# Splitting 62 of 188 weight chunks by GpSimd's transfers, in a float32 decoder trunk on one core

## The chip, the core and the metric

The kernel runs on one core of a Trainium2 chip. The core has a tensor engine (PE, whose weight loads are shown as PEld), a vector engine (DVE), a scalar engine (ACT), GpSimd (POOL) and SyncE (SP), which here only issues transfers. Each engine works through its own queue in order, and semaphores hold an instruction back until what it reads is there. The metric is device time in microseconds (us), the median of several runs.

## The reference

Two post-norm layers over x of 512 tokens by 1024 features, all in float32. A layer is a token mixer and then a gated feed-forward network, each with a residual and a layer norm:

```python
h = x
for i in range(2):
    mix = s5_mixer(h, ...) if i % 2 == 0 else stick_breaking_mixer(h, ...)
    h = layer_norm(ALPHA * h + mix)
    h = layer_norm(ALPHA * h + (silu(h @ w_g) * (h @ w_u)) @ w_down)     # 1024 -> 2816 -> 1024
# s5_mixer: a diagonal complex state-space layer, y = Re(C s) + D u, then
#   val, gate = split(gelu(y) @ w_glu);  (val * sigmoid(gate)) @ w_out
# stick_breaking_mixer: 16 heads of 64, strictly causal, w_qkv and w_o
```

So the order of the weights is w_glu, w_out (state-space layer), gate, up and down of layer 0, w_qkv, w_o (attention), gate, up and down of layer 1.

## The kernel before

**Products in three parts.** The tensor engine multiplies float32r, a rounded float32. Each operand is kept in two float32r parts, the rounded value (wh, xh) and what is left (wl = w - wh, xl), and a product is three: high by high, low by high, high by low. For the gated unit and the gate and up products they are three lines of the profile in this order: L292 (xh by wh), L293 (xh by wl) and L294 (xl by wh).

**The weight stream.** `Weights` brings all weights in as 188 chunks of 128 x 1024 floats (512 KB), in the order in which they are used: 16 of w_glu, 8 of w_out, 44 gate and up and 22 down of layer 0, the attention's 32, and again 44 and 22. `load` issues a transfer on SP's queue into a slot "raw", three chunks ahead of the split. `pump` splits the next chunk: ACT writes wh, the rounded chunk (L228), and DVE, or POOL in some stretches (`l_eng`), writes wl = raw - wh (L231). The raw slot is then given back. `get(i)` returns chunk i's pair, after pumping two chunks further; `done(i)` gives its slots back. All these tiles come from `Ring`: 37 slots of 4 KB a partition, handed out in the order in which they were given back, so that a new tile waits for the last reader of the tile that had the slot before.

**The state-space layer.** Its steps are written out by hand in one string, `SSM_ORDER`, a letter and a block of 16 channel groups each; every engine's queue follows that order. What matters here: g, t and M make the tables g, transpose them (ACT copies them from PSUM to gt, L637) and multiply them with the input (L647); e makes a block's rotation tables e and r8 (POOL, and ACT at L718); r scans the states into s, whose first columns POOL sets to zero (L745); k makes the intra-chunk kernel table (PE L673, ACT's copy L680, and a POOL addition of the skip term to ksb, L466 in the shared helper); y is the output of a block (L766), from s and from xl; p splits one more weight chunk; u1 is one piece of the gated unit's products (L292 to L294), which are spread between the blocks. The 16 w_glu chunks are used in those pieces and in a part behind the layer's steps, the 8 w_out chunks in `proj`.

**The feed-forward layers.** A hidden tile i of 128 takes two chunks, gate and up (`c_gu[l][i]`), 16 steps of three products; 22 tiles, then 22 down chunks (L311 to L313).

Of the kernel before, what the change touches and what calls it, by code (L numbers as in the profile page):

```python
# [45 lines left out]
def glu_items(text):  # L46
    """Tile and quarters of the GLU's products, a word each; the last two stay in PSUM."""
    first = [(int(w[0]), [int(q) for q in w[1:]]) for w in text.split()]
    keep = [i for i, _ in first[-2:]]
    left = lambda i: [q for q in range(4) if not any(i == t and q in qs for t, qs in first)]  # L50
    order = keep + [i for i, _ in first[:-2] if i not in keep]
    order = list(dict.fromkeys(order))
    order += [i for i in range(8) if i not in order]
    return first, [(i, left(i)) for i in order]
# [5 lines left out]
# the steps of the state-space layer, a letter and a block each (see Trunk.ssm)  # L60
# [5 lines left out]
# blocks whose intra-chunk kernels lie in the second half of xl (0) or xh (1)  # L66
# [7 lines left out]
def rsqrt(nc, tmp, var):  # L74
    """(var + EPS) ** -0.5: a seed from the exponent, then Newton's steps; an instruction at a time, the
    result last."""
    V = nc.vector
    mk = lambda n, t=F32: tmp.tile([128, 1], t, tag=f"rq_{n}", name=f"rq_{n}", bufs=2)
    v, m, i, y, t = mk("v"), mk("m"), mk("i", I32), mk("y"), mk("t")
    V.tensor_scalar(out=v, in0=var, scalar1=EPS, scalar2=None, op0=ALU.add)  # L80
    yield
    V.tensor_scalar(out=i, in0=v.bitcast(I32), scalar1=1, scalar2=None, op0=ALU.logical_shift_right)
    V.tensor_scalar(out=m, in0=v, scalar1=-0.5, scalar2=None, op0=ALU.mult)
    yield
    V.tensor_scalar(out=y.bitcast(I32), in0=i, scalar1=-1.0, scalar2=float(0x5F3759DF), op0=ALU.mult, op1=ALU.add)
    yield
    for _ in range(3):
        V.tensor_scalar(out=t, in0=y, scalar1=y, scalar2=m, op0=ALU.mult, op1=ALU.mult)
        yield
        V.tensor_scalar(out=y, in0=t, scalar1=1.5, scalar2=y, op0=ALU.add, op1=ALU.mult)  # L90
        yield y
# [68 lines left out]
class Ring:  # L160
    """SBUF slots of 4 KB a partition, handed out again in the order in which they were given back."""
# [17 lines left out]
class Packer:  # L179
    """Small float32 tiles, packed into slots."""  # L180
# [17 lines left out]
class Weights:  # L198
    """The weight stream: chunks of 1024 floats a partition, split into two float32r parts."""

    def __init__(self, nc, ring):
        self.nc, self.ring = nc, ring
        self.src, self.raw, self.hl = [], {}, {}
        self.loaded = self.split = 0
        self.nraw = 3
        self.h_eng = self.l_eng = None
# [5 lines left out]
    def load(self, upto):  # L212
        while self.loaded <= min(upto, len(self.src) - 1):
            t = self.ring.get("raw", F32)
            self.nc.sync.dma_start(out=t, in_=self.src[self.loaded])
            self.raw[self.loaded] = t
            self.loaded += 1

    def pump(self, upto):
        nc = self.nc  # L220
        upto = min(upto, len(self.src) - 1)
        while self.split <= upto:
            i = self.split
            self.load(i + self.nraw - 1)
            w = self.raw.pop(i)
            h, l = self.ring.get("wh"), self.ring.get("wl")
            if self.h_eng is None:
                nc.scalar.activation(h, w, AF.Copy)  # L228
            else:
                self.h_eng.tensor_copy(h, w)  # L230
            (self.l_eng or nc.vector).tensor_tensor(out=l, in0=w, in1=h.bitcast(F32), op=SUB)  # L231
            self.ring.put(w)
            self.load(i + self.nraw)
            self.hl[i] = (h, l)
            self.split += 1

    def get(self, i, ahead=2):
        self.pump(i + ahead)
        return self.hl[i]
# [5 lines left out]
class Trunk:  # L245
    def __init__(self, tc, io, ctx):
# [14 lines left out]
        # the order in which the weights are used  # L261
# [17 lines left out]
        self.add_ffn(1)  # L279

# [15 lines left out]
    def fm(self, out, hl, cols=slice(0, S)):  # L296
        """out[128 features, cols] = W^T x, the chunk [128, KD, 128] stationary; a step at a time."""
        wh = hl[0].rearrange("p (k m) -> p k m", k=KD)
        wl = hl[1].rearrange("p (k m) -> p k m", k=KD)
        for k in range(KD):  # L300
            self.mm3(out[:, cols], wh[:, k], wl[:, k], self.xh[:, k, cols], self.xl[:, k, cols], k == 0, k == KD - 1)
            yield

    def tm(self, t, hl, sh, sl, first, last, cols=((0, 512), (512, 1024))):
        """The accumulators [128 tokens, 1024] of token tile t += x W, the chunk [128, 1024] moving."""
        ts = slice(t * 128, t * 128 + 128)
        mm = self.nc.tensor.matmul
        acc = self.ps[:, 2 * t:2 * t + 2].rearrange("p a b -> p (a b)")
        for c0, c1 in cols:
            o, c = acc[:, c0:c1], slice(c0, c1)  # L310
            mm(out=o, lhsT=sh[:, ts], rhs=hl[0][:, c], start=first, stop=False)  # L311
            mm(out=o, lhsT=sh[:, ts], rhs=hl[1][:, c], start=False, stop=False)  # L312
            mm(out=o, lhsT=sl[:, ts], rhs=hl[0][:, c], start=False, stop=last)  # L313
# [3 lines left out]
    # xres = LN(ALPHA xres + y W), and the two parts of its transpose  # L317
# [42 lines left out]
    def tail(self, tiles, nxt, out=None, lag=1, fine=False):  # L360
        """Token tiles one after the other: products (tiles[t], a list of steps), LN, transposes late in
        a following tile's products; nxt starts on the first tokens before the last tile is through."""
# [83 lines left out]
    def ffn_first(self, l):  # L446
        """The first two hidden tiles' products, on some of the tokens."""
# [12 lines left out]
    def ssm(self):  # L460
        """The state-space layer, its GLU and output product. State rows are (half of the groups, p);
        blocks of GB groups of either half give the feature tiles b and 4 + b."""
# [11 lines left out]
        # tables of powers: planes (-im, re, im), entries 0 .. 8  # L474
# [54 lines left out]
        # |lambda|^8; exp(i 8 theta); exp(i 8 theta a), exp(i 64 theta a), 0 <= a <= 8  # L529
# [22 lines left out]
        # coef = (lambda_bar - 1) / lambda  # L552
# [7 lines left out]
        def one(gs):  # L560
            """lambda_bar into the table."""
            t = pwt[gs.start]
            tt(t[:, 1, :, 1], mag[:, gs], cs[:, gs], MUL)
            tt(t[:, 2, :, 1], mag[:, gs], sn[:, gs], MUL)
            V.scalar_tensor_tensor(out=t[:, 0, :, 1], in0=sn[:, gs], scalar=-1.0, in1=mag[:, gs], op0=MUL, op1=MUL)
# [13 lines left out]
        def powers(gs):  # L579
            """Powers of lambda, and their products with coef."""  # L580
# [16 lines left out]
        def outer(o, pw, a, gs, part, sign, ns=slice(0, L)):  # L597
            """A part of o = power * a; with sign -1, a and o are (re, -im)."""
# [30 lines left out]
        def p_t(b, c=0):  # L629
            """Transposes of G's part c."""  # L630
# [9 lines left out]
        def p_m(b, c=0):  # L640
            """v = G x, part c."""
# [9 lines left out]
        def p_d(n):  # L651
            """Products that nothing reads: the tensor engine's clock falls when it waits."""
            for _ in range(n):
                nc.tensor.matmul(out=self.ps[:, 7, 0:128], lhsT=ident, rhs=ident, start=True, stop=True)
# [6 lines left out]
        def p_k(b):  # L661
            """K_t = Re(C lambda^t B), laid by lag into the intra-chunk kernel."""
# [37 lines left out]
        def f_e(b):  # L700
            """exp(i 8 theta c) and |lambda|^8, with a break before each chain."""
# [20 lines left out]
        def f_r(b):  # L722
            """S_c = lambda^8 S_{c-1} + v_c, shifted by a chunk."""
# [73 lines left out]
        def glu(i, qs, banks, start=True, stop=True):  # L797
            """Products of the quarters qs (feature tiles q, 4 + q) of val and gate tile i."""
# [90 lines left out]
    def proj(self, chunks, yt, nxt, order=None, begun=0):  # L889
        """Output product of a mixer, y's transpose in slots (high | low), and its LN."""  # L890
# [24 lines left out]
    def att_q(self, bank, v, st):  # L915
        """q / 8, stacked (high; low) for the pair's first head, (low; high) for its second; k's high
        part twice, and its low part."""
# [32 lines left out]
    def attention(self, st0):  # L950
        """Stick-breaking attention; token rows run backwards in time, so that row r attends to the
        rows after it. weight = sigmoid(z) * prod sigmoid(-z) over the keys in between."""
# [10 lines left out]
        # marks: 1 at key = query + 1  # L963
# [8 lines left out]
        def z_(k):  # L972
# [6 lines left out]
            for qb, off, n in segs:  # L979
                # a matmul of fewer than 192 columns takes longer: 64 unused ones before block 3's  # L980
# [22 lines left out]
        def t_(k, part):  # L1003
            p, u = divmod(k, 3)
            s = st[p]
            if "w" not in s:
# [3 lines left out]
                # columns of key block 0: 128, and 64 of zeros  # L1010
# [131 lines left out]
def cpowers(e, t, ta, tb, neg):  # L1142
    """Entries 2 .. 8 of the table t (planes -im, re, im) from entry 1; -im up to entry 2 neg."""
# [32 lines left out]
def host_layout(x, ssm_a_re, ssm_a_im, ssm_log_dt, ssm_b_re, ssm_b_im, ssm_c_re, ssm_c_im, ssm_d,  # L1176
# [7 lines left out]
    # [f, K, M] -> chunks [f // 128 of pairs, part, 128 rows, K/128 * 128]  # L1184
# [14 lines left out]
    # a quarter: [128 rows, feature tiles q and 4 + q, (val, gate), 128 columns of tile i]  # L1199
# [35 lines left out]
```

## Time and profile before

| | |
|---|---|
| Runs | 1273.69, 1273.86, 1273.94; median 1273.86 us |
| Profiled execution | span 1271.4 us from first to last instruction; its own total isn't listed apart from the three runs, which lie 2.3 to 2.5 us above the span |
| Mean granted TensorE clock | 0.978 |
| SP queue's transfers (30.0% of 16 DMA engines' span) | 116.46 MB |
| Read from memory | 112.38 MB, 92 GB/s over the span |
| Transfers issued by POOL | none |

The page's first parts give busy time by engine and by 40 slices of the span; the groups give, for each line, engine and kind of tile, the busy time, the mean of one and the idle time before them with what ended it. A row of the timeline reads: start, length, engine, line, operation, out<-in, shapes, count, and in brackets the engine's idle time before it and what ended that. A row of the waits reads: engine and line, what it waited for, us in total, times, longest.

### The profile page before, as it was taken

What the parts mean: (1) busy time and instruction counts of PE and PEld (TensorE: products, weight loads), DVE (VectorE), ACT (ScalarE), POOL (GpSimd) and SP (SyncE); (2) the same over time, 40 slices, a digit from 0 to 9 for tenths busy, and PEclk for the clock granted to TensorE, in tenths of its full rate; (3) what the DMA queues carried; (4) which work ended last, traced back from release to release, by engine and by line L of the source; (5) the groups of instructions that cost most, each with busy time, mean ns of one, the idle gap of its engine ahead of it and who ended that gap; (6) DMA issues with size and microseconds to landing.
All of it is one profiled execution on the core that took longest, in us unless ns stands there. A gap on an engine that the chain in (4) does not pass through costs nothing.

```text
span 1271.4 us, 16542 instructions
## 1 busy us (share of the span) xinstructions
PE 1189.0 (94%) x6804; PEld 986.4 (78%) x6804; DVE 691.3 (54%) x1030; ACT 421.5 (33%) x588; POOL 224.2 (18%) x217
## 2 busy tenths in 40 slices
PE   3269899999999999999999999999999999999996
PEld 2157678898888888888897788877988888888885
DVE  8859776772333333322777877877623333333236
ACT  1134344233232222322136666553322222223200
POOL 6982206330000000001024222223300000000000
PEclk9589999999999999999999999999999999999998
DMA  4524474132222223434022112122423222234301
GB/s 135 108 42 86 84 259 139 67 132 84 83 77 73 83 83 105 138 125 130 26 75 61 47 60 67 56 94 100 163 70 99 80 70 83 83 115 139 111 18 50
DMA packets 44332, 117.51 MB, mean 92 GB/s; under 512 B 6368, under 2 KB 17760, under 8 KB 44128
## 3 DMA queue, kind: packets, MB, share of 16 engines
q1 hardware_dynamic: 44256, 116.46, 30.0%
q8 instruction: 53, 0.87, 0.3%
q14 instruction: 23, 0.19, 0.1%
HBM read 112.38 MB, written 4.06 MB: 92 GB/s over the span
## 4 chain that ended last, share of the span: by engine, by line
PE 78%; DVE 5%; ACT 2%; POOL 0%; issue 0%; DMA 0%; DVEq 0%; POOLq 0%; ACTq 0%
PE psum L294 16%; PE psum L292 16%; PE psum L293 16%; PE psum L312 8%; PE psum L311 8%; PE psum L313 8%; DVE nb L999 1%; PE psum L1021 1%; PE psum L1086 1%; PE psum L1088 1%; PE psum L1087 1%; PE psum L1037 1%; PE psum L1036 1%; ACT wh L228 1%; DVE wl L231 1%; PE psum L985 1%
## 5 line engine op out<-in xcount | busy, mean ns | idle before, releaser
L293 PE MATMUL psum<-xh,wl 128*128 128x512 f32 (+1 forms) x1056 | 392.9, 373 | 4.8 <-DVE wl L231 4.8
L292 PE MATMUL psum<-xh,wh 128*128 128x512 f32 (+1 forms) x1056 | 395.0, 375 | 0.7 <-ACT xh L287 0.7
L294 PE MATMUL psum<-xl,wh 128*128 128x512 f32 (+1 forms) x1056 | 394.0, 374 | 0.0
L228 ACT ACTIVATE wh<-raw 128x1024 fp32r<-128x1024 f32 x188 | 194.4, 1054 | 231.1 <-PE psum L313 68.7
L231 DVE TENSOR_TENSOR wl<-raw,wh 128x1024 fp32r<-128x1024 f32 x159 | 198.7, 1279 | 126.3 <-ACT wh L228 98.3
L293 PEld LDWEIGHTS psum<-xh,wl 128*128 128x128 f32 x1056 | 198.8, 188 | 40.9 <-DVE wl L231 5.6
L292 PEld LDWEIGHTS psum<-xh,wh 128*128 128x128 f32 x1056 | 198.6, 188 | 38.4 <-issue 2.4
L294 PEld LDWEIGHTS psum<-xl,wh 128*128 128x128 f32 x1056 | 198.4, 188 | 33.5
L410 DVE TENSOR_TENSOR s<-s,psum 128x512 f32<-128x512 f32 x44 | 30.3, 688 | 278.7 <-PE psum L294 278.7
L231 POOL TENSOR_TENSOR wl<-raw,wh 128x1024 fp32r<-128x1024 f32 x29 | 73.2, 2542 | 456.3 <-DMA raw<-w_v 317.2
L313 PE MATMUL psum<-wh,hid 128*128 128x512 f32 x352 | 137.6, 391 | 0.0
L311 PE MATMUL psum<-wh,hid 128*128 128x512 f32 x352 | 137.4, 390 | 0.0
L312 PE MATMUL psum<-wl,hid 128*128 128x512 f32 x352 | 137.4, 390 | 0.0
L287 ACT ACTIVATE hid<-s 128x512 fp32r<-128x512 f32 x44 | 27.7, 629 | 172.4 <-DVE s L410 172.4
L313 PEld LDWEIGHTS psum<-wh,hid 128*128 128x128 f32 x352 | 66.1, 188 | 14.2
L311 PEld LDWEIGHTS psum<-wh,hid 128*128 128x128 f32 x352 | 66.1, 188 | 13.8
L312 PEld LDWEIGHTS psum<-wl,hid 128*128 128x128 f32 x352 | 66.1, 188 | 13.7
L1000 POOL TENSOR_TENSOR be<-be,nb 128x768 f32<-128x768 f32 (+1 forms) x24 | 49.4, 2059 | 97.9 <-DVE nb L999 82.3
L999 DVE TENSOR_TENSOR_SCAN nb<-nb,dm 128x384 f32<-128x384 f32 (+1 forms) x48 | 49.9, 1081 | 9.7 <-ACT nb L994 6.9
L409 ACT ACTIVATE s<-psum 128x512 f32<-128x512 f32 x44 | 26.2, 595 | 74.4 <-PE psum L294 74.3
L636 PE MATMUL psum<-ident,g 128*128 128x128 f32 x64 | 12.1, 350 | 40.9 <-DVE g L466 20.6
L288 DVE TENSOR_TENSOR hid<-s,hid 128x512 fp32r<-128x512 f32 x44 | 30.5, 693 | 32.2 <-ACT hid L287 32.2
(179 smaller groups left out, 1441.6 us busy)
## 6 DMA issues: line engine op xcount, KB each, us to landing
raw<-w_gu SPq DMA_DIRECT2D x88, 512.0 KB, 3.6
raw<-w_down SPq DMA_DIRECT2D x44, 512.0 KB, 3.6
raw<-w_glu SPq DMA_DIRECT2D x16, 512.0 KB, 4.6
raw<-w_qk SPq DMA_DIRECT2D x16, 512.0 KB, 3.6
raw<-w_out SPq DMA_DIRECT2D x8, 512.0 KB, 4.8
raw<-w_v SPq DMA_DIRECT2D x8, 512.0 KB, 3.6
raw<-w_o SPq DMA_DIRECT2D x8, 512.0 KB, 3.5
xres<-xs SPq DMA_DIRECT2D x4, 512.0 KB, 7.3
```

Source lines behind the costliest of these rows:

```text
L228: nc.scalar.activation(h, w, AF.Copy)
L231: (self.l_eng or nc.vector).tensor_tensor(out=l, in0=w, in1=h.bitcast(F32), op=SUB)
L288: self.nc.vector.tensor_tensor(out=l, in0=src, in1=h.bitcast(F32), op=SUB)
L292: mm(out=out, lhsT=sh, rhs=mh, start=first, stop=False)
L293: mm(out=out, lhsT=sl, rhs=mh, start=False, stop=False)
L294: mm(out=out, lhsT=sh, rhs=ml, start=False, stop=last)
L311: mm(out=o, lhsT=sh[:, ts], rhs=hl[0][:, c], start=first, stop=False)
L312: mm(out=o, lhsT=sh[:, ts], rhs=hl[1][:, c], start=False, stop=False)
L313: mm(out=o, lhsT=sl[:, ts], rhs=hl[0][:, c], start=False, stop=last)
L410: nc.vector.tensor_tensor(out=s, in0=s, in1=self.ps[:, b + 1], op=MUL)
L999: V.tensor_tensor_scan(nb[:, h], nb[:, h], dm[u], 0.0, MUL, ADD)
L1000: G_.tensor_tensor(out=be, in0=be, in1=nb, op=MUL)
```

## The change

For 62 chunks (`by_dma`: all of w_glu and w_out, and the gate and up chunks of tiles 3 to 21 of layer 1) there is no raw slot. POOL issues a transfer of the chunk from memory straight into wh, which rounds it to float32r on the way, at the point at which `load` used to issue on SP. `pump` then has ACT write minus wh into wl, and notes that the rest is due. `rest` issues, also from POOL, a transfer that adds the same chunk, read from memory again, to wl: at the next `pump`, or in `get` when the chunk is due. No DVE or POOL subtraction is left for these chunks. The other 126 go as before. (Comments and docstrings are blanked too.)

```diff
     def load(self, upto):
         while self.loaded <= min(upto, len(self.src) - 1):
-            t = self.ring.get("raw", F32)
-            self.nc.sync.dma_start(out=t, in_=self.src[self.loaded])
+            if self.loaded in self.by_dma:
+                t = self.ring.get("wh")
+                self.nc.gpsimd.dma_start(out=t, in_=self.src[self.loaded])
+            else:
+                t = self.ring.get("raw", F32)
+                self.nc.sync.dma_start(out=t, in_=self.src[self.loaded])
             self.raw[self.loaded] = t
             self.loaded += 1
+
+    def rest(self):
+        for i, l in self.minus:
+            self.nc.gpsimd.dma_start(out=l, in_=self.src[i], accum_op=ADD)
+        self.minus = []
...
             self.load(i + self.nraw - 1)
             w = self.raw.pop(i)
+            self.rest()
+            if i in self.by_dma:
+                h, l = w, self.ring.get("wl")
+                nc.scalar.activation(l, h.bitcast(F32), AF.Copy, scale=-1.0)
+                self.minus.append((i, l))
+                self.load(i + self.nraw)
+                self.hl[i] = (h, l)
+                self.split += 1
+                continue
...
     def get(self, i, ahead=2):
         self.pump(i + ahead)
+        if self.minus and i >= self.minus[0][0]:
+            self.rest()
         return self.hl[i]
...
         self.add_ffn(1)
+        ws.by_dma = set(base) | set(self.c_out) | {c for p in self.c_gu[1][3:] for c in p}
```

The changed kernel's lines stand some 23 further down (L660 is before's L637, L768 before's L745, L489 before's L466); L218 is the rounding transfer, L240 ACT's negation, L227 the accumulate. Names end in numbers of the tile.

**The first chunk.** ACT's queue in the early state-space layer, before (wh_38 is chunk 0's high part):

```order
L680 ACTIVATE ksb_22_411<-psum_67 128x512
L637 ACTIVATE gt_30_466<-psum_67 128x512 x2
L228 ACTIVATE wh_38_493<-raw_35_487 128x1024
L718 ACTIVATE r8_43_501<-pk_5_93 128x16x63
L637 ACTIVATE gt_46_515<-psum_67 128x512 x2
L774 ACTIVATE ysb_47_600<-psum_67 128x4x8x16 x2
```

The same place of ACT's queue now (wl_38 is chunk 0's low part, wh_35 its high part):

```order
L703 ACTIVATE ksb_22_411<-psum_67 128x512
L660 ACTIVATE gt_30_466<-psum_67 128x512 x2
L240 ACTIVATE wl_38_493<-wh_35_487 128x1024
L741 ACTIVATE r8_42_499<-pk_5_93 128x16x63
L660 ACTIVATE gt_45_513<-psum_67 128x512 x2
L797 ACTIVATE ysb_46_598<-psum_67 128x4x8x16 x2
```

ACT's order is the same; its source is now a transfer that POOL issues. POOL's queue around that point, before (s_29 is block 0's states, e and eu block 1's rotation tables):

```order
L1144 TENSOR_TENSOR scr_1_79<-pk_5_93 128x2x96 x2
L1144 TENSOR_TENSOR pk_5_93<-scr_1_79 128x48x4
L745 MEMSET s_29_460 128x16
L466 TENSOR_TENSOR e_41_499<-pk_5_93,pk_4_90 128x512
L466 TENSOR_TENSOR eu_42_500<-pk_5_93,pk_4_90 128x512
```

And POOL's queue there now:

```order
L1167 TENSOR_TENSOR scr_1_79<-pk_5_93 128x2x96 x2
L1167 TENSOR_TENSOR pk_5_93<-scr_1_79 128x48x4
L768 MEMSET s_29_460 128x16
L218 DMA wh_35_487<-w_glu 128x1024
L218 DMA wh_36_489<-w_glu 128x1024
L218 DMA wh_37_491<-w_glu 128x1024
L218 DMA wh_39_495<-w_glu 128x1024
L489 TENSOR_TENSOR e_40_497<-pk_5_93,pk_4_90 128x512
L489 TENSOR_TENSOR eu_41_498<-pk_5_93,pk_4_90 128x512
```

The first four chunks' transfers moved from SP's queue, where nothing stood ahead of them, to behind POOL's power tables and the memset of s.

**The middle of the layer.** POOL's queue before, from block 1's kernel table (ksb_52) to block 2's (ksb_86):

```order
L466 TENSOR_TENSOR ksb_52_691<-pk_2_80,ksb_52_691 128x4x16
L745 MEMSET s_60_729 128x16
L466 TENSOR_TENSOR e_71_821<-pk_5_93,pk_4_90 128x512
L466 TENSOR_TENSOR eu_72_822<-pk_5_93,pk_4_90 128x512
L466 TENSOR_TENSOR e_71_821<-pk_5_93,pk_4_90 128x512
L466 TENSOR_TENSOR eu_72_822<-pk_5_93,pk_4_90 128x512
L466 TENSOR_TENSOR e_71_821<-e_71_821,eu_72_822 128x512 x2
L719 MEMSET r8_73_823 128x16
L466 TENSOR_TENSOR ksb_86_1048<-pk_2_80,ksb_86_1048 128x4x16
```

POOL's queue now from block 1's kernel table on (wl_38 and wl_54 are the low parts of chunks 0 and 1):

```order
L489 TENSOR_TENSOR ksb_51_689<-pk_2_80,ksb_51_689 128x4x16
L227 DMA wl_38_493<-w_glu 128x1024
L218 DMA wh_55_717<-w_glu 128x1024
L768 MEMSET s_58_726 128x16
L227 DMA wl_54_715<-w_glu 128x1024
L218 DMA wh_65_810<-w_glu 128x1024
L489 TENSOR_TENSOR e_68_817<-pk_5_93,pk_4_90 128x512
```

The accumulate of chunk 0 now stands directly behind that addition. POOL's queue around block 2's kernel table (wl_64, wl_78 and wl_88 are chunks 2, 3 and 4, wh_145 a w_out chunk):

```order
L227 DMA wl_64_808<-w_glu 128x1024
L218 DMA wh_79_950<-w_glu 128x1024
L218 DMA wh_145_1758<-w_out 128x1024
L489 TENSOR_TENSOR ksb_82_1043<-pk_2_80,ksb_82_1043 128x4x16
L227 DMA wl_78_948<-w_glu 128x1024
L218 DMA wh_89_1085<-w_glu 128x1024
L227 DMA wl_88_1083<-w_glu 128x1024
```

Chunk 3's accumulate stands behind the addition, and that behind a w_out load. POOL's queue around block 3's kernel table (wl_101 is chunk 5):

```order
L218 DMA wh_142_1721<-w_out 128x1024
L218 DMA wh_140_1716<-w_out 128x1024
L227 DMA wl_101_1236<-w_glu 128x1024
L218 DMA wh_104_1244<-w_glu 128x1024
L489 TENSOR_TENSOR ksb_105_1310<-pk_2_80,ksb_105_1310 128x4x16
```

The accumulates stand between POOL's own steps: behind a kernel table's addition, or behind a load whose slot another engine has to give back first (wh_145's by DVE's u, wh_140's by the last products of block 3's kernel table).

**The last layer.** POOL's queue had no rows there before. Now, from the load of a tile on (wl_642 and wl_644 are tile 4's low parts, wh_668 is the high part of a later tile):

```order
L218 DMA wh_665_7670<-w_gu 128x1024
L218 DMA wh_668_7705<-w_gu 128x1024
L227 DMA wl_642_7383<-w_gu 128x1024
L227 DMA wl_644_7412<-w_gu 128x1024
L218 DMA wh_670_7734<-w_gu 128x1024
L227 DMA wl_647_7447<-w_gu 128x1024
```

Each accumulate stands behind a load, and that load waits until PE gives the slot back.

More of the change, by code (lines that the diff above doesn't have):

```diff
@@ L205, in __init__ @@
         self.nraw = 3
+        self.by_dma, self.minus = set(), []
         self.h_eng = self.l_eng = None
```

## The prediction

> **What bounds the kernel now.** I read the page first: the engines' shares and the row of slices.
>
> ```profile
> span 1271.4 us, 16542 instructions
> PE 1189.0 (94%) x6804; PEld 986.4 (78%) x6804; DVE 691.3 (54%) x1030; ACT 421.5 (33%) x588; POOL 224.2 (18%) x217
> PE   3269899999999999999999999999999999999996
> ```
>
> TensorE is 94% busy; its idle time lies in the first six or so of 40 slices, the state-space layer. Next the busy time by stage (columns: length, busy time of PE, PEld, DVE, ACT, POOL with counts, then clock, DMA share, GB/s).
>
> ```profile
> 81.00:172.00 91.00, 81.40 (x990) 62.98 (x992) 75.84 (x59) 42.24 (x60) 27.38 (x23) 0.96 0.49 101
> 960.00:1100.00 140.00, 140.00 (x613) 114.85 (x613) 46.28 (x50) 39.75 (x52) 0.00 (x0) 1.00 0.27 83
> ```
>
> From 960 to 1100 (the last feed-forward layer) PE never stops and DVE works 46.28 of 140 us: no relief of DVE can be worth anything there. From 81 to 172 PE leaves 9.6 us idle and DVE is 83% busy. So the whole effect is decided by what PE waits for before about 172 us. Those waits are:
>
> ```profile
> PE psum L766 <- POOL s L745: 11.4, 1, 11.4
> PE psum L293 <- DVE wl L231: 4.8, 2, 4.3
> PE psum L766 <- DVE s L466: 2.7, 2, 1.9
> ```
>
> Only the last two rows are waits for DVE; together 7.5 us is the most that less DVE work in this stage could give.
>
> **What is taken away.**
>
> ```profile
> L228 ACT ACTIVATE wh<-raw 128x1024 fp32r<-128x1024 f32 x188 | 194.4, 1054 | 231.1 <-PE psum L313 68.7
> L231 DVE TENSOR_TENSOR wl<-raw,wh 128x1024 fp32r<-128x1024 f32 x159 | 198.7, 1279 | 126.3 <-ACT wh L228 98.3
> raw<-w_glu SPq DMA_DIRECT2D x16, 512.0 KB, 4.6
> xres<-xs SPq DMA_DIRECT2D x4, 512.0 KB, 7.3
> L215 SPq DMA_DIRECT2D raw<-w_glu x16: 327/387/497, 42.1 to 178.7; - x16
> 190.59 2.42 POOL L231 TENSOR_TENSOR wl<-raw,wh 128x1024 fp32r<-128x1024 f32 x1 [26.20 <-DVE wl L231]
> ```
>
> 62 of 188 chunks lose their subtraction: 52 on DVE (159 become 107; 52 x 1.28 = 66 us of DVE) and 10 on POOL (10 x 2.42 = 24 us). ACT keeps 188 passes of the same shape, which now write minus the rounded chunk. SP loses 62 loads; POOL gains 124 transfers, and each of the 62 chunks is read from memory twice, +32.5 MB. The last layer reads 83 GB/s now. While its gate and up chunks pass it would read at most twice that, 166.
>
> **The unknown prices.** No transfer from POOL's queue is in this trace, so two durations and one issue time are bounded.
> - The rounding transfer, issue to landing. The nearest row is a plain load of the same 512 KB from the same tensor; its landings here were:
>
> ```profile
> DMA to landing us min/median/max: 3.3/4.5/9.5
> ```
>
>  I take the median, 4.5 us, bounds 3.3 and 9.5.
> - The accumulate. It reads the tile back besides reading memory; I put it midway between that median and the slowest kind on the page, the 7.3 us of the xres load: 5.9 us, same bounds.
> - POOL's time to issue one: between SP's 0.33 us and the 2.42 us that POOL takes to go over the whole tile; I take 1.0, nearer to the issue row, since an issue doesn't touch the data.
>
> **Place A, the first chunk.** Before, ACT rounds chunk 0 at 50.75, from a load at 42.1 us. Now its source is a transfer that stands in POOL's row directly behind the memset of s.
>
> ```profile
> 50.75 1.05 ACT L228 ACTIVATE wh<-raw 128x1024 fp32r<-128x1024 f32 x1
> 51.69 1.03 ACT L718 ACTIVATE r<-pk 128x1008 f32<-128x1008 f32 x1
> 54.30 0.60 ACT L637 ACTIVATE gt<-psum 128x512 f32<-128x512 f32 x1 [0.26 <-PE psum L636]
> 55.05 1.98 PE L647 MATMUL psum<-xres,gt 128*64 128x64 f32 x32
> 71.45 0.12 POOL L745 MEMSET s<- 128x16 f32 x1
> 71.63 1.12 PE L766 MATMUL psum<-h,s 64*64 64x128 f32 x8 [11.43 <-POOL s L745]
> 72.68 0.69 PE L766 MATMUL psum<-xl,xres 128*64 128x128 f32 x4
> 88.00 1.07 ACT L637 ACTIVATE gt<-psum 128x512 f32<-128x512 f32 x2
> ```
>
> ACT's queue is in order: behind the pass over chunk 0 stand r8 and the two copies to gt, PE's block-1 products wait for gt, and y0 stands behind them on PE. All of this used to be over by 57 us, in the shadow of the memset at 71.45; now it starts there. 71.57 + 4.5 landing = 76.1; pass 0.94 (51.69 - 50.75) 77.0; r8 1.0, 78.0; two gt copies 1.07, 79.1; products 1.98, 81.1; the part of y0 that needs only xl and xres 0.69, 81.8. y0 started at 71.63: 10.1 late, less 0.8 that I allow because some of the products overlap the second copy. **A: +9.3 us.** The four issues also put POOL's e tables 4 us back, less than PE's own delay.
>
> **Place B, the first gated-unit product.** The accumulate of chunk 0 stands behind the kernel-table addition ksb on POOL.
>
> ```profile
> 86.58 0.58 ACT L680 ACTIVATE ksb<-psum 128x512 f32<-128x512 f32 x1
> 87.24 1.10 POOL L466 TENSOR_TENSOR ksb<-pk,ksb 128x64 f32<-128x64 f32 x1 [1.24 <-ACT ksb L680]
> 88.38 0.39 PE L293 MATMUL psum<-xh,wl 128*128 128x512 f32 x1
> 128.68 0.39 PE L294 MATMUL psum<-xl,wh 128*128 128x512 f32 x1
> 128.91 0.40 PE L292 MATMUL psum<-xh,wh 128*128 128x512 f32 x1
> 133.62 0.80 PE L293 MATMUL psum<-xh,wl 128*128 128x512 f32 x1 [4.32 <-DVE wl L231]
> 137.05 0.39 PE L292 MATMUL psum<-xh,wh 128*128 128x512 f32 x1
> ```
>
> ksb ends at 88.34 and PE's product with wl is at 88.38: there is no slack. 88.34 + 5.9 = 94.24, 5.9 us of waiting. A pause also costs afterwards: behind the 4.32 us one, eight products took 3.43 us (133.62 to 137.05), against 0.23 from one to the next at full pace (128.68 to 128.91): 3.43 - 1.84 = 1.6. **B: +7.5.**
>
> **Place C.** y1's wait for DVE goes, since DVE runs ahead by four subtractions.
>
> ```profile
> 104.69 0.94 PE L766 MATMUL psum<-h,s 64*64 64x128 f32 x8 [1.89 <-DVE s L466]
> ```
>
> **C: -1.9.**
>
> **Place D, chunks 3 and 4.** POOL first issues a w_out load into a slot that DVE's u gives back, then ksb, then chunk 3's accumulate.
>
> ```profile
> 121.35 0.80 POOL L466 TENSOR_TENSOR ksb<-pk,ksb 128x64 f32<-128x64 f32 x1 [16.03 <-ACT ksb L680]
> 121.89 1.34 DVE L466 TENSOR_TENSOR u<-pk,bb 128x1024 f32<-128x1024 f32 x1
> 123.64 0.39 PE L293 MATMUL psum<-xh,wl 128*128 128x512 f32 x1
> ```
>
> u ends at 123.23; + 1.0 + 0.8 + 5.9 = 130.9 against 123.64: 7.3, and 1.6 for the pace. In return the 4.3 us stall at 133.62 and its 1.6 go (chunk 4's accumulate is issued right behind, in the new wait). **D: +3.0.**
>
> **Place E, chunk 5.** POOL issues a w_out load whose slot comes free only with PE's last products of block 3's kernel tables, and chunk 5's accumulate stands behind it.
>
> ```profile
> 151.78 0.57 PE L673 MATMUL psum<-h,g 64*32 64x112 f32 x16
> 155.65 0.50 PE L293 MATMUL psum<-xh,wl 128*128 128x512 f32 x1 [0.49 <-DVE wl L231]
> 170.61 0.94 PE L766 MATMUL psum<-h,s 64*64 64x128 f32 x8 [0.81 <-DVE s L466]
> ```
>
> 152.35 + 1.0 + 5.9 = 159.25 against 155.65: 3.6 + 1.6. **E: +5.2.** The wait of 0.81 at 170.61 is DVE's: **F: -0.8.** From there PE has a backlog, and the later chunks are split ahead.
>
> **The last layer.** Each gate-and-up tile of 16 x 3 products takes about 11 us (48 x 0.23). POOL's queue there holds, word for word in the order of rows, a rounding load that waits for the products of tile i-2 to end, then the accumulates of tile i.
>
> ```profile
> 934.13 1.99 ACT L228 ACTIVATE wh<-raw 128x1024 fp32r<-128x1024 f32 x2
> 943.82 0.39 PE L293 MATMUL psum<-xh,wl 128*128 128x512 f32 x1
> ```
>
> The first of ACT's two passes over tile 4 ends at about 935.2, PE wants the tile at 943.82: 8.6 us for the accumulate, against 5.9. And four issues a tile may take 2.75 us each before POOL is the bound. **Term: 0**; the cover is those 8.6 us, and if it is gone, the excess comes 18 times.
>
> **The sum.** 9.3 + 7.5 - 1.9 + 3.0 + 5.2 - 0.8 = +22.3: span 1271.4 becomes 1293.7. Between span and reported time lie 2.5 us (median 1273.86), so about 1296. The places are added as if POOL's and ACT's rows shift along with PE; every one is anchored to an event of the same chain.
> Low ends (3.3, 3.3, 0.33, no pace loss): 8.1 + 3.3 - 1.9 - 0.3 + 0.3 - 0.8 = +8.7, 1282.6. High ends (9.5, 9.5, 2.42): 14.3 + 11.1 - 1.9 + 8.0 + 10.2 - 0.8 = +40.9, 1314.8, and (9.5 - 8.6) x 18 = 16 more in the last layer, 1331.
>
> The Trainium skill, "DMA: Bandwidth & Descriptors", section "Anatomy of one DMA — SWDGE (gpsimd) path", fits a transfer from GpSimd's queue as about 2.0 us plus its bytes over 436e3 per us; for 524,288 bytes that is an estimate of 3.2 us for either transfer. By it the sum would be 8.0 + 3.2 - 1.9 + 0.3 + 0.9 - 0.8 = +9.7, about 1283.6, the second rival below. The trace's plain loads never landed under 3.3 and at the median took 4.5, so I hold it for a floor.
>
> **Rivals.**
> - *The accumulates don't keep up in the last layer* (0.17). Each us above 8.6 costs 18 us there; at 10 us: 1.4 x 18 = 25, and 4.1 more at B, D and E each, 12.3: 1273.9 + 22.3 + 12.3 + 25 = about 1333. For it: the bytes of two reads, a read back and a write, and the 9.5 us that a plain load has taken. Against: in that layer the DMA engines are 27% busy.
> - *The transfers are quick* (0.10): all near 3.3 us, about 1283. Place A remains, because it comes from the row order, not from the length of a transfer. Against: w_glu's median of 4.5 in that very stage.
> - *The relief of DVE decides* (0.03 faster, 0.02 the same). The waits for wl and s (4.3, 0.5, 1.9, 0.8 and 1.6 of pace) go, 9.1 us: about 1265. That needs chunk 0 rounded before ACT reaches it at 50.75, so issued by about 46; POOL's row puts it after 71.45. It turns to a gain where A, B, D and E cost under 9 together; A alone at its low end is 8.1.
>
> **How the numbers follow.** The forecast has 0.68. The predicted time is its sum, 1296; its own range is 1282 to 1315. The range for 8 in 10 goes on to 1326, into the first rival, leaving out the rest of that rival (about 0.12) and the last one. A difference under 0.2%, 2.5 us, can't be told from none. Slower: 0.68 + 0.17 + 0.10 = 0.95; same 0.02; faster 0.03.
>
> **What the changed profile would show.** A: a wait of y0's group (or of the block-1 products before it) for ACT's gt, and chunk 0's rounding issued near 71.6; if it is issued before 50, A falls. B, D, E: PE's L293 products waiting for a DMA into wl near 98, 140 and 170 us, of 4 to 8 us each. C, F: no waits for s at L766. Last layer: PE without gaps for 140 us in a stretch behind 980; a gap of the same size in each of 18 tiles shows the first rival. The prediction is wrong if the accumulate lands outside 3.3 to 9.5 us, if POOL's issue is above 2.42, or if POOL's rows wait on something that I haven't followed.

## The result, and the profile after

The changed kernel takes 1314.62 us (median of 4 runs, 1313.23 to 1315.76) against 1273.78 for the kernel before beside it: ratio 1.0321, 95% interval 1.0309 to 1.0334. That is 40.8 us slower; the forecast was 22 slower, with this time just inside the high end of its range (1282 to 1315). The page of the changed kernel:

```profile
span 1312.5 us, 16633 instructions
PE 1196.7 (91%) x6804; PEld 991.9 (76%) x6804; DVE 621.5 (47%) x978; ACT 420.9 (32%) x588; POOL 283.9 (22%) x331
...
DMA  4318779923222222344320212213477787864301
...
q0 software_dynamic: 17856, 65.02, 21.6%
q1 hardware_dynamic: 35328, 83.95, 21.6%
...
wh<-w_gu POOLq DMA_DIRECT2D x38, 512.0 KB, 6.0
wl<-w_gu POOLq DMA_DIRECT2D x38, 512.0 KB, 7.1
wh<-w_glu POOLq DMA_DIRECT2D x16, 512.0 KB, 7.0
wl<-w_glu POOLq DMA_DIRECT2D x16, 512.0 KB, 10.2
...
wh<-w_out POOLq DMA_DIRECT2D x8, 512.0 KB, 12.7
```

DVE has 70 us less work, and the kernel is slower all the same. The row of DMA shares has a plateau that wasn't there before: 8 7 7 9 9 in slices 4 to 8 (from about 98 to 262 us), and 7s and 8s in the last layer. POOL's 124 transfers (q0) occupy the 16 transfer engines for 21.6% of 1312.5 us, 2.29 us each on average; SP's transfers before took 30.0% of 1271.4 for 116.46 MB, 1.72 us for each 512 KB. The last column of the issues is the median from issue to landing: 6 to 13 us, where the plain loads of weights took 3.5 to 4.8 in the kernel before.

TensorE's waits (engine and line, what it waited for, total, times, longest):

```profile
PE psum L670 <- ACT gt L660: 23.4, 1, 23.4
...
PE psum L316 <- DMA wl<-w_glu: 17.4, 3, 7.0
PE psum L335 <- DMA wl<-w_out: 10.0, 1, 10.0
```

The first row takes the place of the old 11.4 us wait for POOL's memset; it begins earlier on PE, so only part of it is new. The three waits for wl<-w_glu are the forecast's places B, D and E. The wait for w_out has no counterpart in the forecast. The rows of PE's timeline at these places:

```profile
80.98 1.12 PE L789 MATMUL psum<-h,s 64*64 64x128 f32 x8
104.77 0.79 PE L316 MATMUL psum<-xh,wl 128*128 128x512 f32 x1 [5.56 <-DMA wl<-w_glu]
145.99 0.80 PE L316 MATMUL psum<-xh,wl 128*128 128x512 f32 x1 [7.04 <-DMA wl<-w_glu]
179.18 0.80 PE L316 MATMUL psum<-xh,wl 128*128 128x512 f32 x1 [4.84 <-DMA wl<-w_glu]
265.34 0.80 PE L335 MATMUL psum<-wl,zt 128*128 128x512 f32 x1 [9.99 <-DMA wl<-w_out]
```

PE issues the same 6804 products in both kernels, in the same order but for two, so each product's start can be set against its start before. How far the changed kernel lies behind, by place, is worked out from the two traces. "Pace" is what PE loses in slower products behind a pause: behind the wait that ends at 104.77 the granted clock was 0.50 from 104.8 to 109.6, and 1.00 again from 110 on.

| Place | start before | start after | behind | forecast | measured |
|---|---|---|---|---|---|
| A, block 0's output | 71.63 | 80.98 | 9.4 | +9.3 | +9.4 |
| up to the first gated-unit product | 88.03 | 98.36 | 10.3 | 0 | +1.0 |
| B, chunk 0's low part | 88.38 | 104.77 | 18.7 with pace | +7.5 | +8.4 |
| C, block 1's output | 108.76 | 124.24 | 15.5 | -1.9 | -3.2 |
| D, chunk 3, and chunk 4's old wait gone | 136.78 | 155.43 | 18.7 | +3.0 | +3.2 |
| E, chunk 5 | 155.65 | 179.18 | 26.0 with pace | +5.2 | +7.3 |
| F, block 3's output | 170.61 | 197.12 | 26.5 | -0.8 | +0.6 |
| to the last of the gated unit | 206.62 | 235.60 | 29.0 | 0 | +2.5 |
| G, w_out | 226.09 | 265.34 | 41.6 with pace | 0 | +12.6 |
| from there to the end | | | 41 | 0 | 0 |

The two products that moved are of the gated unit, stood behind block 3's output before and stand ahead of it now. They lie in the row of F and hide its gain: from the products of block 3's output that need no s (169.36 before) to those that do (170.61) PE gains 0.9.

The windows show the stage of G and the last layer (columns as in the prediction; a packet counts whole where it starts, so the share of a full stretch can read a little over 1). First the end of the state-space layer in the kernel before, then the changed kernel:

```profile
182.00:236.00 54.00, 54.00 (x238) 44.34 (x237) 36.61 (x35) 28.42 (x34) 28.83 (x12) 1.00 0.48 174
```

```profile
205.00:265.00 60.00, 47.87 (x210) 38.15 (x208) 20.39 (x28) 28.27 (x36) 18.23 (x21) 0.96 1.07 289
...
1000.00:1100.00 100.00, 100.00 (x439) 82.14 (x438) 12.42 (x18) 28.14 (x36) 24.36 (x33) 1.00 0.78 169
```

From 205 to 265 the DMA share is 1.07: the transfer engines are full, and PE is idle for 12.1 us. The last w_out chunk shows both its transfers late: its rounding load, issued at 240.38, lands at 253.89, and its accumulate, issued at 255.32 behind ACT's negation, at 265.30. In the last layer the engines are 78% busy, against 27% before, and PE never stops.

### The profile page after: what moved, and what is told of

The parts are those of the page before. It is cut to its first block, busy times and chain, and to the rows that moved or that the text cites. A ratio compares the mean times of both kernels' runs of the same rounds, so it can differ in the third digit from the quotient of the medians.

```text
span 1312.5 us, 16633 instructions
## 1 busy us (share of the span) xinstructions
PE 1196.7 (91%) x6804; PEld 991.9 (76%) x6804; DVE 621.5 (47%) x978; ACT 420.9 (32%) x588; POOL 283.9 (22%) x331
## 3 DMA queue, kind: packets, MB, share of 16 engines
q0 software_dynamic: 17856, 65.02, 21.6%
q1 hardware_dynamic: 35328, 83.95, 21.6%
## 4 chain that ended last, share of the span: by engine, by line
PE 77%; POOL 6%; DVE 6%; issue 5%; DMA 4%; ACT 3%; SPq 0%; DVEq 0%; POOLq 0%; ACTq 0%
PE psum L317 15%; PE psum L316 15%; PE psum L315 15%; PE psum L335 8%; PE psum L336 8%; PE psum L334 8%; POOL scr L1167 2%; DVE nb L1022 1%; DMA wh<-w_out 1%; PE psum L789 1%; PE psum L1044 1%; POOL pk L1167 1%; DMA wl<-w_glu 1%; PE psum L1109 1%; DMA wl<-w_out 1%
## 5 line engine op out<-in xcount | busy, mean ns | idle before, releaser
L316 PEld LDWEIGHTS psum<-xh,wl 128*128 128x128 f32 x1056 | 200.4, 190 | 54.4 <-DMA wl<-w_glu 18.7
L248 ACT ACTIVATE wh<-raw 128x1024 fp32r<-128x1024 f32 x126 | 131.9, 1057 | 224.3 <-PE psum L336 68.4
L251 DVE TENSOR_TENSOR wl<-raw,wh 128x1024 fp32r<-128x1024 f32 x107 | 134.8, 1286 | 107.0 <-ACT wh L248 79.1
L251 POOL TENSOR_TENSOR wl<-raw,wh 128x1024 fp32r<-128x1024 f32 x19 | 47.6, 2522 | 411.8 <-DMA raw<-w_v 317.2
L240 ACT ACTIVATE wl<-wh 128x1024 fp32r<-128x1024 f32 x62 | 62.7, 1046 | 50.2 <-DMA wh<-w_glu 38.0
L659 PE MATMUL psum<-ident,g 128*128 128x128 f32 x64 | 13.0, 370 | 42.2 <-DVE g L489 20.6
L227 POOL DMA_DIRECT2D wl<-w_gu x38 | 33.8, 899 | 77.2 <-ACT wl L240 75.1
## 6 DMA issues: line engine op xcount, KB each, us to landing
wl<-w_glu POOLq DMA_DIRECT2D x16, 512.0 KB, 10.2
wh<-w_out POOLq DMA_DIRECT2D x8, 512.0 KB, 12.7
```

The costliest lines, as they stand in the source:

```text
L240: nc.scalar.activation(l, h.bitcast(F32), AF.Copy, scale=-1.0)
L316: mm(out=out, lhsT=sl, rhs=mh, start=False, stop=False)
```

## Experiments

**The last layer alone.**

```diff
-ws.by_dma = set(base) | set(self.c_out) | {c for p in self.c_gu[1][3:] for c in p}
+ws.by_dma = {c for p in self.c_gu[1][3:] for c in p}
```

> Only the 38 gate and up chunks of the last layer are split by transfers; w_glu and w_out go as before. Theory (the whole loss lies before 275 us, the accumulates of the last layer land within their 8.6 us): 1273.8, within 1 us of the kernel before, no wait of TensorE for a low part between 940 and 1185 us. Rival (the last layer costs something that the delays don't show, its POOL queue or its doubled reads): 1277 to 1290.

1273.02 us, ratio 0.9996 (0.9987 to 1.0005): no difference, as forecast. The window of the last layer in this run, to be read beside the row of the kernel before that the prediction shows:

```profile
960.00:1100.00 140.00, 140.00 (x613) 114.99 (x612) 17.95 (x26) 39.78 (x52) 31.33 (x43) 1.00 0.79 175
```

DVE's work there falls from 46.28 to 17.95 us and the time doesn't move. Relieving an engine that has slack was worth nothing here, and the price, transfer engines at 79% where they were at 27%, is hidden too.

**Without w_out.**

```diff
+ws.by_dma = set(base) | {c for p in self.c_gu[1][3:] for c in p}
```

> The 8 w_out chunks go back to SP's loads and to subtractions; all else is as changed. Theory (the last w_out chunk's accumulate costs 10.3 us and 2.4 of pace at its products, and a w_out load ahead of chunk 3's accumulate on POOL costs 2 at the third wait): 1314.6 - 12.7 - 2 = 1300. Rival (the transfer engines are so full from w_glu alone that the same wait comes at another chunk): 1308 to 1315.

1307.73 us (1.0269, 1.0254 to 1.0285): 6.9 us come back, half of what the theory said, and just below what the rival said. The wait of 10.0 is gone and D's wait is 2 us shorter as expected (5.1 for 7.0), but new waits stand in its place (rows of PE's waits):

```profile
PE psum L316 <- DMA wl<-w_glu: 16.9, 5, 5.3
PE psum L804 <- ACT ysb L797: 3.9, 2, 3.2
...
PE psum L334 <- ACT wh L248: 2.0, 1, 2.0
PE psum L335 <- POOL wl L251: 1.9, 1, 1.9
```

E stays (a wait of 4.95), although no w_out load stands ahead of chunk 5's accumulate any more. The transfer engines are still full (a share of 0.97 from 175 to 205 us and of 1.02 from 205 to 235).

**Without chunk 0.**

```diff
+ws.by_dma = set(base[1:]) | set(self.c_out) | {c for p in self.c_gu[1][3:] for c in p}
```

> Chunk 0 alone goes back to SP's load, ACT's rounding and DVE's subtraction; the other 61 are as changed. Theory (both the late start of block 0's output, 9.4, and the first gated-unit product's wait, 6.1 with 2.3 of pace, belong to this one chunk, with some 1 us between them): 1314.6 - 18.7 = 1296, block 0's output at 71.6 again. Rival (the delay of the first part hides another one behind it, such as later chunks that come no earlier): less than 10 us gained, 1305 or more.

1298.94 us (1.0199, 1.0185 to 1.0213), 15.7 back. Block 0's output starts at 71.26 again, and the first gated-unit product doesn't wait: one chunk of 62 held A and B. Of the 3 us that are missing to 18.7, 1.55 are a wait for chunk 1, at 96.18, that chunk 0's had hidden; the rest isn't put down to one place.

**Half of the late accumulates' bytes.** The second half of these low parts is left at minus the high part.

```diff
-            self.nc.gpsimd.dma_start(out=l, in_=self.src[i], accum_op=ADD)
+            n = 512 if 8 <= i < 24 else 1024
+            self.nc.gpsimd.dma_start(out=l[:, :n], in_=self.src[i][:, :n], accum_op=ADD)
```

> The accumulates of chunks 8 to 23 (half of w_glu, all of w_out) add only the first 512 of 1024 columns: half of their bytes, the same queues and the same order; the other half of these low parts stays at minus the high part. Theory S (from 205 to 265 us the 16 transfer engines are full, so the last w_out accumulate waits for others): 4.2 MB less at some 285 GB/s is 14.7 us of their time, so the wait of 10.0 for the last w_out chunk falls to under 3: 1302 to 1305. Theory Q (it is late because its load is issued late, behind slots and POOL's order): the wait stays at 8 or more, 1311 to 1314.

1299.66 us (1.0209, 1.0192 to 1.0226): 15.0 back, somewhat more than theory S said. The order on every queue is unchanged, and A, B, D and E are as in the changed kernel; PE's list of waits has none for w_out, and the same window reads:

```profile
205.00:265.00 60.00, 60.00 (x268) 49.16 (x267) 29.15 (x38) 30.38 (x37) 24.66 (x23) 1.00 0.84 233
```

PE is busy for all 60 us as soon as the transfer engines aren't full (0.84). So G is the transfer engines' throughput, not the place in a queue; theory Q falls.

**The accumulate at once.**

```diff
                 self.minus.append((i, l))
+                self.rest()
```

> The accumulate of a chunk is issued right behind ACT's negation of it, not at the next pump; the same 62 chunks. Theory (the waits for low parts of chunks 0 and 3 come from where the accumulate stands in POOL's queue): chunk 0's now stands ahead of block 1's rotation tables and lands by 85, so its wait of 5.6 with 2.3 of pace goes; chunk 3's stands ahead of the w_out load and the kernel table, so its 7.0 with 2.3 goes, but chunk 4 (behind a part addition) waits some 4 to 6 as in the kernel before; the late start of 9.4, chunk 5's wait (ACT's late negation) and the w_out wait stay: 1300 to 1304. Rival (the length of the transfers decides, not their place): 1311 to 1315.

1317.58 us (1.0341, 1.0315 to 1.0366), no gain, and above the range of theory and rival alike. The waits at B and D are gone (at the product that started at 133.62 before, the kernel is 8.0 us behind, where the changed kernel is 20.2), so their cause, the place in POOL's queue, is borne out. But from 155 to 178 us on before's scale this kernel falls from 10 to 30 us behind, where the changed kernel falls from 19 to 26: some 13 us come on top. At w_out a wait of 8.2 stays. Two rows of POOL's timeline in that stretch:

```profile
193.61 0.89 POOL L227 DMA_DIRECT2D wl<-w_glu  x1 [9.13 <-ACT wl L240]
194.21 0.85 POOL L218 DMA_DIRECT2D wh<-w_glu  x1
```

An accumulate at once waits at the head of POOL's queue for ACT, and the next chunk's load stands behind it; the kernel that put the accumulate a step later let the load go first. Here that load landed at 201.00, and PE, which had waited 5.6 us for it, went on at 201.13. How much of the other 7 us is such order and how much is full transfer engines wasn't separated.

**Two or three chunks, early accumulate.** Both have the line of the run before, and:

```diff
+ws.by_dma = {base[2], base[4]}        # the first;  set(base[2:5]) the second
```

> Only chunks 2 and 4 of w_glu are split by transfers, the accumulate right behind the negation; everything else as in the kernel before. Theory (a few chunks, loaded ahead and away from the first product, take DVE off the path): the wait of 4.3 with 1.6 of pace for chunk 4 shrinks to 0 to 3, and block 1's output waits less for DVE (1.9): 1266 to 1271. Rival (POOL's queue makes new waits even with two): 1274 or more.

> As the run with chunks 2 and 4, with chunk 3 too. Theory: chunk 3's accumulate, ahead of block 2's kernel table on POOL, lands before its product, and DVE has one subtraction less: 1265 to 1270, equal to the run with two within 2. Rival (chunk 3's product waits as in the changed kernel, since its negation is late on ACT): 1274 to 1279.

1279.86 (1.0046, 1.0031 to 1.0061) and 1279.61 (1.0043, 1.0026 to 1.0060): some 0.5% slower, outside the theory in both runs. The rival of the first (POOL's queue makes new waits) fits; in the second chunk 3 didn't wait, so its rival isn't the cause. The first loss is not a wait for a transfer: block 1's output waits 3.9 us for DVE's s, 1.9 before. POOL's accumulate of chunk 2 waited for ACT until 100 us, the rotation tables stood behind it, and they then ran at the same time as DVE's additions of s. DVE's timeline and POOL's, with chunks 2 and 4:

```profile
100.83 7.95 DVE L490 TENSOR_TENSOR s<-s,w 128x504 f32<-128x504 f32 x2
```

```profile
100.00 0.90 POOL L227 DMA_DIRECT2D wl<-w_glu  x1 [10.35 <-ACT wl L240]
100.60 1.45 POOL L490 TENSOR_TENSOR e<-pk,pk 128x512 f32<-128x512 f32 x1
```

**The same two, accumulate at the next pump; and chunks 1, 2, 4.** The accumulate stands as in the change.

```diff
+ws.by_dma = {base[2], base[4]}        # the first;  {base[1], base[2], base[4]} the second
```

> Chunks 2 and 4 alone by transfers, the accumulate at the next pump as in the change (it stands behind the rotation tables of block 3 on POOL, not ahead of them). Theory (in the run with the early accumulate, POOL's tables were held until 100 us and then ran beside DVE's additions of s, which took 7.95 instead of 1.28): the tables run at 88 to 99 again, DVE's additions take 1.3, block 1's output isn't late, and chunk 4 waits 2 to 4 instead of 4.3: 1271 to 1274. Rival (it is the transfers themselves that slow DVE): 1278 to 1281 again.

> Chunks 1, 2 and 4 by transfers, accumulates at the next pump. Theory: with chunk 1's subtraction gone DVE reaches block 1's states 1.2 earlier and its wait of 1.9 goes, chunk 1's product waits some 1.8 for its accumulate, chunk 4 waits 2 to 4 instead of 4.3 and 1.6: 1269 to 1273, level with the kernel before or under it by up to 0.4%. Rival (chunk 1's accumulate or the tables behind it make a larger wait): 1275 or more.

1275.09 (1.0013, 1.0004 to 1.0022) and 1276.51 (1.0025, 1.0016 to 1.0035), the first 1 us above its theory's range, the second in its rival's. With chunks 2 and 4, POOL's tables are out of the way in time and the additions take their usual length:

```profile
104.07 1.28 DVE L489 TENSOR_TENSOR s<-s,w 128x504 f32<-128x504 f32 x2
```

The row is DVE's timeline with chunks 2 and 4. Block 1's output is on time, as the theory said, and some 4.5 us of the loss are back. What is left is chunk 4, whose accumulate POOL issues behind a part addition (row of PE's timeline with chunks 2 and 4):

```profile
134.24 0.80 PE L316 MATMUL psum<-xh,wl 128*128 128x512 f32 x1 [6.20 <-DMA wl<-w_glu]
```

PE waits 6.2 us, where DVE's subtraction cost 4.3 and the theory said 2 to 4. With chunk 1 as well, chunk 1's accumulate costs 1.7, as the theory said, but the wait for chunk 4 is 6.7. No version with transfers in the state-space layer beat the kernel before, and the last layer alone is level with it.

**Without chunks 0, 3, 5 and w_out.**

```diff
+ws.by_dma = set(base) - {base[j] for j in (0, 3, 5)} | {c for p in self.c_gu[1][3:] for c in p}
```

> Chunks 0, 3 and 5 of w_glu and all of w_out go back to SP, ACT and DVE; 13 w_glu chunks and the last layer's 38 stay with the transfers. Theory (the loss is at the first chunk, the three accumulates that are late, and the w_out stage): all five are gone, and 1.8 for chunk 1 and some pace stay: 1270 to 1278. Rival (other chunks become late in their place, since the transfer engines are full from 175 us on and a later accumulate stands in the same row): 1282 to 1292.

1291.02 us (1.0141, 1.0127 to 1.0155), in the rival's range. At the product of 153.26 (before) this kernel is 0.3 us behind, so what A, B and D cost is gone. From there to 247 us it loses 18 us, in waits of 3.4 for a late accumulate (at 164.86), 3.4 for ACT's ysb (at 190.44), and smaller ones, with the pace behind them, while the transfer engines are full from 160 to 205:

```profile
160.00:205.00 45.00, 37.50 (x209) 27.95 (x208) 9.61 (x7) 13.62 (x16) 14.51 (x14) 0.89 0.96 245
```

Then the same with the accumulates of chunks 6 to 15 halved (their second half stays at minus the high part):

```diff
+            n = 512 if 6 <= i < 24 else 1024
+            self.nc.gpsimd.dma_start(out=l[:, :n], in_=self.src[i][:, :n], accum_op=ADD)
```

> As the run without chunks 0, 3, 5 and w_out, but the accumulates of chunks 6 to 15 add only the first 512 of 1024 columns: the same instructions in the same order on every queue, 2.6 MB less to move; the other half of these low parts stays at minus the high part. Theory S (the 18 us lost between 160 and 247 us are the transfer engines' throughput): 2.6 MB at some 300 GB/s is 8.7 us, so 6 to 10 us come back: 1281 to 1285. Theory Q (they come from the order on POOL's and ACT's queues, in which the accumulates wait for other engines): 1288 to 1292.

1285.01 us (1.0097, 1.0076 to 1.0118): 6.0 us back, the low end of what S said, with every queue's order the same; the distance behind at the end of that stretch falls from 18.0 to 11.9. So traffic is part of it. Waits of 1.7 for an accumulate, 2.0 for a rounding load, 1.5 for ACT's ysb and 1.9 for a subtraction on POOL remain, and how much of these is traffic too stays open.

## Why the prediction was right, and where it fell short

- **What bounds the kernel, and what DVE's relief is worth: right.** The last layer's term of 0 was measured alone at 0.9996. Its cover of 8.6 us was enough: the accumulates there took 7.1 at the median; 6 of 38 took more than 8.6, up to 11.2, and PE didn't stop for them either. Four issues a tile took 2 x 0.55 + 2 x 0.88 = 2.9 us of 11 (rows below), so POOL never came near its bound. One reading is short: the same view of PE's waits before has 20.6 us for DVE's g (L636), which the prediction leaves out of the waits for DVE. They are 20.6 in the changed kernel too, so the sum doesn't suffer.

```profile
L218 POOL DMA_DIRECT2D wh<-w_gu x38: 527/551/1297, 920.5 to 1128.5; - x38
L227 POOL DMA_DIRECT2D wl<-w_gu x38: 860/880/1292, 941.5 to 1164.8; - x38
```

- **A: right in place and size** (9.4 for 9.3). Chunk 0's rounding was issued at 71.66 and ACT's pass over it began at 76.13, forecast 76.1; without that chunk the term is gone.
- **B, D: right in place, close in size.** The accumulates for which PE waited were issued at 97.86 and 139.58 and PE went on at 104.77 and 145.99: 6.9 and 6.4 us, where 5.9 was taken. The early accumulate removed both. The pace behind a pause cost 2.3 and not 1.6 each.
- **E: right in place and nearly in size, wrong in what ends last.** The w_out load did wait for PE's products of block 3's table until 171.53, but chunk 5's accumulate, issued at 173.86, waited for ACT's negation, which ran later still:

```profile
171.53 0.53 POOL L218 DMA_DIRECT2D wh<-w_out  x1 [8.99 <-PE psum L696]
173.86 0.89 POOL L227 DMA_DIRECT2D wl<-w_glu  x1 [1.80 <-ACT wl L240]
```

 Without any w_out load, the wait was still there.
- **C and F: both gains came**, C with 1.4 of pace on top, F with 0.9 (hidden in its row by the two products that moved).
- **The step that failed** is the sentence behind F, "From there PE has a backlog, and the later chunks are split ahead." It took POOL's transfers one by one, each with a landing time, and never summed what they ask of the 16 engines. With that it held that the whole effect is decided before about 172 us; G's product started at 226 before. By the shares of the two pages of the profile, 48 transfers of 2.29 us are 110 us of all 16 engines in the state-space layer, in place of 24 x 1.72 = 41, and 44 of them come late, between 98 and 265 us. From 205 to 265 the engines are full, an accumulate issued at 255.32 lands at 265.3, and w_out costs 12.6 us that the forecast has at 0. Halving the late accumulates' bytes alone took it away. With 3.5 more at E and F, 2.5 behind them and some 0.8 in sum at the other places, this is the difference between 22.3 and 41.6.
- **The landing bound of 9.5 us was too low.** The median was 10.2 for w_glu's accumulates and 12.1 for w_out's, and the longest took 20.1 (row of the full list of issues):

```profile
wl<-w_out POOLq DMA_DIRECT2D x8, 512.0 KB, 12.1
```

 An accumulate outside 3.3 to 9.5 us is one of the prediction's own signs of being wrong. The high end of the sum, 1314.8, met the result by another way than its own: it had B, D and E longer, and the trace has them as forecast, with G on top. So the range held by luck, not for the reasons given for its upper part, and the sum itself, 22.3, has little more than half of the 41 us.
- By the page of the Trainium skill that the prediction weighed ("DMA: Bandwidth & Descriptors", "Anatomy of one DMA — SWDGE (gpsimd) path") a transfer would take 3.2 us, an estimate. Here the medians are 6.0 to 12.7; the case by that formula, 1283.6, fell with them.

## What to carry to other kernels

When work moves from an engine to transfers, sum the transfers' time on the 16 engines by stage, not only each one's landing: the accumulates landed after 7.1 us at the median in the last layer, with a share of 0.78, and after 10 to 20 where the share was 1.07. Look for the chunk that stands at the head of an in-order queue, since one of 62 held some 16 of 41 us here. And cost the relief where the relieved engine is waited for; where the bottleneck engine never stops, it is worth nothing.

## What the hardware showed that I had not expected

- It is the addition that is dear for the transfer engines, not the rounding. Of q0's packets in order of start 144 belong to a transfer; set against POOL's issues in order, they give 1.66 us of all 16 engines for a rounding transfer of 512 KB and 2.91 for one that adds, on average of 62 each. In the kernel before a plain load of 512 KB takes 1.66 (packets from 300 to 500 us) and 1.68 (960 to 1100). In the last layer the bytes doubled and the engines' share nearly tripled, 0.27 to 0.78.
- DVE's two additions of 128x504 took 7.95 us beside POOL's table products, and 1.28 without them (rows above). In the kernel before, the additions w of 128x512 took 3.27 while POOL made its tables (first row), and 1.29 in the run with chunks 2 and 4 and the early accumulate, where it made them later (second row). The Trainium skill, "SBUF — State Buffer", section "Who interferes with whom", states that a DVE instruction with two inputs in SBUF contends with a GpSimd instruction that reads SBUF; the rows agree, though no run here tried it alone. So in that run a transfer that held POOL's queue slowed DVE later, by moving POOL's work to a worse time.

```profile
94.90 3.27 DVE L466 TENSOR_TENSOR w<-w,x 128x512 f32<-128x512 f32 x2
```

```profile
94.74 1.29 DVE L490 TENSOR_TENSOR w<-w,x 128x512 f32<-128x512 f32 x2
```
